# A hybrid trunk on one core: the power of qs, the clearing of Z and the additions on G are put in other places of the queues

## The chip, the core and the metric

The kernel runs on one core of a Trainium2 chip. The metric is device time in microseconds for one whole execution: lower is better. A core has TensorE (PE), whose queue also loads weights (PEld), VectorE (DVE), ScalarE (ACT), GpSimd (POOL) and SyncE (SP). Each takes its instructions in the order in which they were queued for it, and waits for other engines and for DMAs through semaphores.

## What is computed

Two layers of a decoder trunk in float32, sequence 512, width 1024. Each layer has a mixer (eight heads of dilated attention beside four heads of a gated delta rule, one input and one output projection) and a gated feed-forward part. The part around the change is the delta rule. Cut from the reference:

```python
qkv = jax.nn.silu(causal_dwconv(dn_qkv, dn_conv_w)).astype(jnp.float32)
...
q = q * lax.rsqrt(jnp.sum(q * q, axis=-1, keepdims=True) + EPS) * (K ** -0.5)
k = k * lax.rsqrt(jnp.sum(k * k, axis=-1, keepdims=True) + EPS)
...
g = jnp.cumsum(g, axis=-1)
decay = jnp.exp(jnp.where(tril, g[..., :, None] - g[..., None, :], -jnp.inf))
A = jnp.where(strict, jnp.einsum('bhnik,bhnjk->bhnij', kb, k) * decay, 0.0)
T = lax.linalg.triangular_solve(A + eye, jnp.broadcast_to(eye, A.shape), left_side=True,
                                lower=True, unit_diagonal=True)
...
def step(state, xs):
    v_new = u_i - jnp.einsum('bhck,bhkv->bhcv', w_i, state)
    o = jnp.einsum('bhck,bhkv->bhcv', q_i, state) + jnp.einsum('bhij,bhjv->bhiv', qk_i, v_new)
    state = state * gl[..., None, None] + jnp.einsum('bhck,bhcv->bhkv', k_i, v_new)
...
dn_out = (rms_norm(o, dn_norm_w) * jax.nn.silu(z)).reshape(B, S, DELTA_V_WIDTH).astype(h.dtype)
```

## The kernel before

Tokens are handled as four tiles of 128 (t = 0 to 3), which are also the chunks of the delta rule. A dense product is made as three products of split operands, a high and a low part (hh and hl of the activations, wh and wl of the weights); wh is a rounded copy by ScalarE, wl the rest by VectorE, from a loaded piece st. Dense products gather in PSUM tiles pm (4 buffers), all small ones in pw (4 buffers).

Every instruction goes through one helper (line 54), so all rows name L54 and are told apart by their tiles. A tile scheduler orders each engine's queue by a priority: `prio` sets the level, `weave` mixes streams of work by their share of progress (dense projections, `prepare`, `attention`, `invert`, `scan`). Dense work has a late level, the delta rule's chain an early one. What the scheduler finds ready first by its own costs stands first, so an edit also moves instructions that it doesn't name.

The delta rule in order, with the names in the rows:

- `key` and `conv_silu` (lines 373 to 387): a short convolution into acc, ScalarE's tanh into kT, and one VectorE instruction kT<-kT,acc that finishes a head's key. TensorE then transposes it (pw<-ident,kT).
- `decay` (to line 453): the running sums of the decay go to DRAM (dG), and one DMA for each chunk spreads them back over partitions into G. SP issues these.
- `prepare` (lines 461 to 524): norms of the keys (ssk, bb, bd, and sk by a power on GpSimd); for each chunk and head VectorE adds ng and a mask to G (G<-G,ng,dmask), ScalarE takes the exponential, and U is made of G and a product of keys. 32 x 32 diagonal blocks of U (Lb) are inverted by a chain on GpSimd (Xt, X), and the result goes to DRAM (dX).
- `invert` (lines 526 to 582): for two chunks at once, GpSimd issues the DMA of zc from dX and clears zt and the two Z; VectorE transposes zc's 32 x 32 blocks into Z; GpSimd copies zc into zt; TensorE builds the larger blocks from Z and UT (pw<-Z,UT, then pw<-PB,zt).
- `query` and `project2` (lines 637 to 677): the sums of squares of the queries, qs (128 x 16), become rsqrt(sum + 4 EPS) / sqrt(128) by an addition on VectorE, a power of -0.5 on GpSimd and a multiplication on VectorE.
- `scan` (lines 769 to 818): chunk by chunk R<-pw,neg,Vt, TensorE's R,Z into y, the new state S<-S,egl,pw, and the output o.
- `normed` (lines 830 to 845): ScalarE's sums of squares of o scaled by qs (junk<-o,qs in the trace; four for each chunk, into os), os scaled by VectorE, the power of on GpSimd, and dno.

Of the kernel before, what the change touches and what calls it, by code (L numbers as in the profile page):

```python
# [12 lines left out]
AF = mybir.ActivationFunctionType  # L13
OP = mybir.AluOpType
# [3 lines left out]
P = 128  # L18
# [7 lines left out]
H = 4  # L26
DK = 128
FF = 2816
NF = 22
EPS = 1e-6  # L30
NB = 32
# [40 lines left out]
class Engine:  # L72
# [3 lines left out]
    def __getattr__(self, name):  # L76
        f = getattr(self._engine, name)
        return lambda *args, **kwargs: self._engines.issue(f, self._pe, args, kwargs)


def run(gen):
# [5 lines left out]
def hybrid_trunk(ctx: ExitStack, tc: tile.TileContext, a, out):  # L87
    nc = Engines(tc)
# [10 lines left out]
    def const(name, shape):  # L99
        t = cp.tile(shape, F32, name=name)  # L100
        nc.sync.dma_start(t, a[name])
        return t
# [12 lines left out]
    with prio(2.5):  # L115
        cw = const("cw", [P, NL, 12, 4])
        dmask = const("dmask", [P, P])
# [14 lines left out]
    def big(name, dtype=F32, shape=(P, T), tag="b2", bufs=None):  # L132
        return bp.tile(list(shape), dtype, name=name, tag=tag, bufs=bufs)

    def ev(name, dtype=F32, shape=(P, T)):
        return big(name, dtype, shape, "ev", 4)

    def am(name, dtype=F32, shape=(P, T)):
        return big(name, dtype, shape, "am", 4)

    def pair(name, shape=(P, 2, T)):
        return big(name, F32, shape, "b4", 2)
# [19 lines left out]
    def ps4(name="pw", shape=(P, 4, P)):  # L162
        return pw.tile(list(shape), F32, name=name, tag="pw")
# [47 lines left out]
    def square_sum(src, acc, scale=1.0, tag="junk"):  # L211
        junk = sp.tile([P, D if tag == "junk" else T], BF, name="junk", tag=tag, bufs=1)
        nc.scalar.activation(junk[:, :src.shape[-1]], src, AF.Square, scale=scale, accum_out=acc)
# [122 lines left out]
    def s16(name):  # L336
        return sp.tile([P, 16], F32, name=name, bufs=1)

    def v3(t_):
        return t_.rearrange("p (t h) -> p t h", h=H)  # L340
# [4 lines left out]
    for l in range(NL):  # L345
# [27 lines left out]
        def conv_silu(cb, ps, dst):  # L373

            acc = ev("acc")
            nc.scalar.activation(acc, ps, AF.Copy, scale=cw[:, l, cb, 3:4])
            for j in range(1, 4):
                nc.vector.scalar_tensor_tensor(acc[:, j:], ps[:, :T - j], cw[:, l, cb, 3 - j:4 - j], acc[:, j:],
                                               op0=OP.mult, op1=OP.add)
            nc.scalar.activation(dst, acc, AF.Tanh, scale=0.5)  # L380
            nc.vector.scalar_tensor_tensor(dst, dst, 1.0, acc, op0=OP.add, op1=OP.mult)

        kT, qT, Kt, Vt = [], [], [], []

        def key(h, ps):
            kT.append(big("kT"))
            conv_silu(4 + h, ps, kT[h])


        bet, bb, bd, ng, eg, neg, egl, ssk, gr = (s16(n) for n in ("bet", "bb", "bd", "ng", "eg", "neg", "egl", "ssk",  # L390
                                                                    "gr"))
        sk, qs = s16("sk"), s16("qs")
        Gs, UT, Z = [], [], []
# [67 lines left out]
        def prepare():  # L461
            for h in range(H):
                pk = ps4()
                for t in range(NT):
                    nc.tensor.transpose(pk[:, t, :], kT[h][:, t * P:(t + 1) * P], ident)
                Kt.append(big("Kt", shape=(P, NT, P)))
                for t in range(NT):
                    square_sum(pk[:, t, :], v3(ssk)[:, t, h:h + 1])
                sk_h, bb_h, bd_h = (v3(v)[:, :, h] for v in (ssk, bb, bd))
                nc.vector.tensor_scalar(sk_h, sk_h, 4 * EPS, None, op0=OP.add)  # L470
                nc.vector.reciprocal(bb_h, sk_h)
                nc.vector.tensor_tensor(bb_h, bb_h, v3(bet)[:, :, h], op=OP.mult)
                nc.vector.tensor_tensor(bd_h, bd_h, bb_h, op=OP.mult)
                for t in range(NT):
                    i = t * H + h
                    nc.scalar.activation(Kt[h][:, t, :], pk[:, t, :], AF.Copy, scale=bd[:, i:i + 1])
                yield
            nc.vector.tensor_scalar(sk, ssk, 0.25, None, op0=OP.mult)
            nc.gpsimd.tensor_tensor(sk, sk, pexp[:, :16], op=OP.pow)
            yield  # L480

            Lb = pair("Lb", (64, NB, NB))
            X = pair("X", (64, NB, NB))
            nc.sync.dma_start(X.rearrange("p a b -> p (a b)"), a["eye32"])
            for t in range(NT):
                G = Gs[t]
                for h in range(H):
                    i = t * H + h
                    nc.vector.scalar_tensor_tensor(G[:, h, :], G[:, h, :], ng[:, i:i + 1], dmask,
                                                   op0=OP.add, op1=OP.add)  # L490
                nc.scalar.activation(G, G, AF.Exp)
                pu = ps4()
                U = am("U", shape=(P, H, P))
                for h in range(H):
                    ks = kT[h][:, t * P:(t + 1) * P]
                    nc.tensor.matmul(pu[:, h, :], ks, ks, start=True, stop=True)
                for h in range(H):
                    i = t * H + h
                    nc.vector.scalar_tensor_tensor(U[:, h, :], pu[:, h, :], bb[:, i:i + 1], G[:, h, :],
                                                   op0=OP.mult, op1=OP.mult)  # L500
                nc.sync.dma_start(dU[t, :P * H * P].rearrange("(p n) -> p n", p=P), U.rearrange("p h i -> p (h i)"))
                pt = ps4()
                for h in range(H):
                    nc.tensor.transpose(pt[:, h, :], U[:, h, :], ident)
                UT.append(big("UT", shape=(P, H, P)))
                nc.scalar.activation(UT[t], pt, AF.Copy)
                yield

            for h in range(H):
                src = bass.AP(tensor=dU.tensor, offset=dU.offset + h * P,  # L510
                              ap=[[NB * H * P + NB, 16], [H * P, NB], [1, NB]])
                nc.sync.dma_start(Lb[h * 16:h * 16 + 16], src)
            for j in range(NB - 1):
                n = NB - 1 - j
                tmp = xp.tile([64, 256], F32, name="Xt", tag="Xt")
                tv = tmp[:, :n * (j + 1)].rearrange("p (n m) -> p n m", n=n)
                nc.gpsimd.tensor_tensor(tv, Lb[:, j, j + 1:].unsqueeze(2).to_broadcast([64, n, j + 1]),
                                        X[:, j, None, :j + 1].to_broadcast([64, n, j + 1]), op=OP.mult)
                nc.gpsimd.tensor_tensor(X[:, j + 1:, :j + 1], X[:, j + 1:, :j + 1], tv, op=OP.subtract)
                if j % 4 == 3:  # L520
                    yield
            for h in range(H):
                dst = bass.AP(tensor=dX.tensor, offset=dX.offset + h * NB, ap=[[NB * P, 16], [P, NB], [1, NB]])
                nc.gpsimd.dma_start(dst, X[h * 16:h * 16 + 16])

        def invert():

            for t0 in range(0, NT, 2):
                ts_ = range(t0, t0 + 2)
                zc = am("zc", shape=(P, 2, H, NB))  # L530
                nc.gpsimd.dma_start(zc.rearrange("p t h i -> p t (h i)"),
                                    dX[t0 * P:(t0 + 2) * P, :].rearrange("(t p) n -> p t n", p=P))
                zt = xp.tile([64, 2, H, 64], F32, name="zt")
                nc.gpsimd.memset(zt, 0.0)
                for t in ts_:
                    Z.append(big("Z", shape=(P, H, P)))
                    nc.gpsimd.memset(Z[t], 0.0)
                for t in ts_:
                    for r in range(0, P, NB):
                        nc.vector.transpose(Z[t][r:r + NB, :, r:r + NB], zc[r:r + NB, t - t0])  # L540
                for r in (0, NB):
                    nc.gpsimd.tensor_copy(zt[r:r + NB, :, :, r:r + NB], zc[r:r + NB])
                pp = ps4(shape=(P, 2, H, NB))
                pb = ev("PB", shape=(P, 2, H, NB))
                for r in (0, 64):
# [16 lines left out]
                for t in ts_:  # L562
                    for r in (0, 64):
                        nc.vector.tensor_scalar(Z[t][r:r + 32, :, r + 32:r + 64], po[r:r + 32, t - t0], -1.0, None,
                                                op0=OP.mult)
# [60 lines left out]
        def at_proj(s, evac):  # L626
            return tok_proj(lambda pc: load_w(a["w_at"][l, s, pc], [2, T]), 4, act_h, 2, evac)
# [42 lines left out]
        def project2():  # L670
            yield from chan_proj(lambda b: a["w_dn"][l, 8 + b], 4, 0, delta_value)
            yield from chan_proj(lambda b: a["w_dn"][l, b], 4, 0, query, (), lambda b: nc.gpsimd if b > 1 else None)
            with prio(*CHAIN):
                nc.vector.tensor_scalar(qs, qs, 4 * EPS, None, op0=OP.add)
                nc.gpsimd.tensor_tensor(qs, qs, pexp[:, 16:], op=OP.pow)
                nc.vector.tensor_scalar(qs, qs, DK ** -0.5, None, op0=OP.mult)
            yield from at_proj(3, gate)

        heads = []
# [425 lines left out]
```

## Time and profile before

| | us |
|---|---|
| median of 3 runs | 1341.43 |
| range of these runs | 1341.21 to 1342.85 |
| profiled execution | 1338.06 |
| its span in the trace | 1336.3 |
| TensorE busy | 1298.1 |
| VectorE busy | 1005.6 |
| ScalarE busy | 724.8 |
| GpSimd busy | 182.5 |

A row of a timeline reads: start, duration (from the first start to the last end, where several instructions are joined), engine, line, operation, output<-inputs, shapes, count, and in brackets the idle time of the engine before it with what ended that. A row of TensorE's waits reads: the waiting work <- what it waited for: us in total, times, longest. Engines start the next instruction a little before the printed end of the one ahead, so the distance of two starts is what an instruction costs its queue.

### The profile page before, as it was taken

How to read it: one execution, taken by the hardware profiler on the slowest of the kernel's cores; microseconds unless marked ns; L12 is line 12 of the kernel's file. 1: busy time of each engine (PE TensorE's matmuls, PEld its weight loads, DVE VectorE, ACT ScalarE, POOL GpSimd, SP SyncE). 2: the span in 40 equal slices, each digit the busy share in tenths (PEclk: the TensorE clock that was granted, in tenths of full speed). 3: DMA queues.
4: the chain of work that ended last, by engine and by line, in shares of the span. 5: the costliest groups of instructions: out<-in, count | busy, mean ns of one | idle time of the engine just before them, and what ended most of it. 6: DMA issues, size and time to landing. Idle time of an engine off the chain costs nothing.

```text
span 1336.3 us, 19288 instructions
## 1 busy us (share of the span) xinstructions
PE 1298.1 (97%) x6892; PEld 1082.3 (81%) x6892; DVE 1005.6 (75%) x1940; ACT 724.8 (54%) x1458; POOL 182.5 (14%) x230
## 2 busy tenths in 40 slices
PE   8999999999999999999999999999999999999997
PEld 7787878888888888888777877888888888888876
DVE  6756878868576778788777668889667667888885
ACT  5635966755333444467546359667553334444673
POOL 0019410101000000030010293002110000001201
PEclk9999999999999999999999999999999999999999
DMA  7233211253366566356652332203435565653664
GB/s 238 85 103 96 71 52 37 67 177 120 139 228 222 183 220 206 116 178 187 212 174 72 110 96 61 66 17 115 138 127 192 195 228 190 222 187 109 199 187 160
DMA packets 75425, 193.14 MB, mean 145 GB/s; under 512 B 13345, under 2 KB 13889, under 8 KB 75330
## 3 DMA queue, kind: packets, MB, share of 16 engines
q1 hardware_dynamic: 74882, 190.87, 44.4%
q0 software_dynamic: 448, 1.05, 0.4%
q8 instruction: 54, 0.88, 0.3%
q14 instruction: 41, 0.34, 0.1%
HBM read 161.99 MB, written 29.90 MB: 144 GB/s over the span
## 4 chain that ended last, share of the span: by engine, by line
PE 79%; DVE 8%; ACT 5%; DMA 3%; POOL 2%; issue 2%; SPq 0%; POOLq 0%; DVEq 0%; ACTq 0%
PE pm L54 66%; PE pw L54 13%; DVE wl L54 2%; DVE xs L54 1%; ACT wh L54 1%; DVE x L54 1%; POOL nr L54 1%; ACT junk L54 1%; ACT sc L54 1%; DVE hl L54 1%; DMA st<-in_w_f 1%; POOL pr L54 1%; DVE xf L54 1%; ACT Vt L54 0%; DVE KL L54 0%
## 5 line engine op out<-in xcount | busy, mean ns | idle before, releaser
L54 DVE TENSOR_TENSOR wl<-st,wh 128x1024 fp32r<-128x1024 f32 (+1 forms) x250 | 282.3, 1135 | 165.6 <-ACT wh L54 164.5
L54 PE MATMUL pm<-hh,wh 128*128 128x512 f32 (+1 forms) x1024 | 372.5, 366 | 4.7 <-ACT hh L54 4.7
L54 ACT ACTIVATE wh<-st 128x1024 fp32r<-128x1024 f32 (+1 forms) x254 | 245.5, 971 | 239.2 <-PE pm L54 217.5
L54 PE MATMUL pm<-hh,wl 128*128 128x512 f32 (+1 forms) x1024 | 373.0, 366 | 1.1 <-DVE wl L54 1.1
L54 PE MATMUL pm<-hl,wh 128*128 128x512 f32 (+1 forms) x1024 | 373.6, 367 | 0.0
L54 PEld LDWEIGHTS pm<-hh,wh 128*128 128x128 f32 x1024 | 193.7, 190 | 35.4 <-ACT hh L54 6.0
L54 PEld LDWEIGHTS pm<-hh,wl 128*128 128x128 f32 x1024 | 194.3, 191 | 30.8 <-DVE wl L54 1.3
L54 PEld LDWEIGHTS pm<-hl,wh 128*128 128x128 f32 x1024 | 194.4, 191 | 29.2
L54 PE MATMUL pm<-wh,xf 128*128 128x512 f32 x528 | 164.4, 390 | 0.0
L54 PE MATMUL pm<-wh,hh 128*128 128x512 f32 x384 | 153.4, 402 | 0.0
L54 PE MATMUL pm<-wl,hh 128*128 128x512 f32 x384 | 152.5, 399 | 0.0
L54 PE MATMUL pm<-wh,hl 128*128 128x512 f32 x384 | 151.3, 396 | 0.0
L54 DVE SCALAR_TENSOR_TENSOR fgu<-pm,fw,fgu 128x511 f32<-128x511 f32 (+1 forms) x176 | 131.2, 746 | 22.0 <-ACT fgu L54 19.9
L54 PEld LDWEIGHTS pm<-wh,xf 128*128 128x128 f32 x528 | 99.1, 188 | 21.2 <-ACT e L54 0.6
L54 PE MATMUL pm<-wl,xf 128*128 128x512 f32 x264 | 103.6, 392 | 0.5 <-DVE wl L54 0.5
L54 POOL TENSOR_TENSOR g<-g 128x256 f32<-128x256 f32 x22 | 25.4, 1173 | 493.1 <-DVE xf L54 493.1
L54 PEld LDWEIGHTS pm<-wh,hl 128*128 128x128 f32 x384 | 72.4, 189 | 14.2
L54 PEld LDWEIGHTS pm<-wh,hh 128*128 128x128 f32 x384 | 72.0, 188 | 14.4 <-DVE zs L54 0.6
L54 PEld LDWEIGHTS pm<-wl,hh 128*128 128x128 f32 x384 | 72.5, 189 | 13.7 <-DVE wl L54 0.8
L54 ACT ACTIVATE xf<-g 128x256 fp32r<-128x256 f32 x154 | 60.4, 411 | 33.9 <-PE pm L54 22.3
L54 ACT ACTIVATE fgu<-fgu 128x512 f32<-128x512 f32 x44 | 27.8, 632 | 91.8 <-DVE fgu L54 89.2
L54 ACT ACTIVATE fgu<-pm,fb,fw 128x512 f32<-128x512 f32 x88 | 66.9, 761 | 18.6 <-PE pm L54 18.6
(228 smaller groups left out, 1798.7 us busy)
## 6 DMA issues: line engine op xcount, KB each, us to landing
st<-in_w_f SPq DMA_DIRECT2D x118, 512.0 KB, 3.7
ws<-in_w_f SPq DMA_DIRECT2D x88, 256.0 KB, 4.6
T<-ws SPq DMA_DIRECT2D x66, 256.0 KB, 2.3
st<-in_w_at SPq DMA_DIRECT2D x32, 512.0 KB, 3.8
st<-T SPq DMA_DIRECT2D x30, 512.0 KB, 4.1
st<-in_w_dn SPq DMA_DIRECT2D x24, 512.0 KB, 3.8
st<-in_w_out SPq DMA_DIRECT2D x16, 512.0 KB, 3.7
U<-ws SPq DMA_DIRECT2D x22, 256.0 KB, 2.3
```

The lines of the kernel that those rows point to most:

```text
L54: r = f(*args, **kwargs)
```

## The change

Three edits in the mixer. In the **power of qs**, VectorE adds 4 EPS and multiplies by 128 in one instruction ahead of GpSimd's power, and the multiplication behind the power is gone. **Z** of the first two chunks is taken and cleared at the end of `prepare`; the other two are cleared in `invert` as before, and the zt copies are done by ScalarE. The **additions on G** carry a rule that they are queued behind the last key's final instruction.

```diff
+@contextmanager
+def behind(tc, ins):
+    if ins is None:
+        yield
+    else:
+        with tc.issue_after(ins.ins):
+            yield
...
             nc.scalar.activation(dst, acc, AF.Tanh, scale=0.5)
-            nc.vector.scalar_tensor_tensor(dst, dst, 1.0, acc, op0=OP.add, op1=OP.mult)
-
-        kT, qT, Kt, Vt = [], [], [], []
+            return nc.vector.scalar_tensor_tensor(dst, dst, 1.0, acc, op0=OP.add, op1=OP.mult)
+
+        kT, qT, Kt, Vt, keyed = [], [], [], [], []
 
         def key(h, ps):
             kT.append(big("kT"))
-            conv_silu(4 + h, ps, kT[h])
+            keyed.append(conv_silu(4 + h, ps, kT[h]))
...
-                for h in range(H):
-                    i = t * H + h
-                    nc.vector.scalar_tensor_tensor(G[:, h, :], G[:, h, :], ng[:, i:i + 1], dmask,
-                                                   op0=OP.add, op1=OP.add)
+                with behind(tc, keyed[-1]):
+                    for h in range(H):
+                        i = t * H + h
+                        nc.vector.scalar_tensor_tensor(G[:, h, :], G[:, h, :], ng[:, i:i + 1], dmask,
+                                                       op0=OP.add, op1=OP.add)
...
                 nc.gpsimd.dma_start(dst, X[h * 16:h * 16 + 16])
+            cleared(range(2))
+
+        def cleared(ts_):
+            for t in ts_:
+                Z.append(big("Z", shape=(P, H, P)))
+                nc.gpsimd.memset(Z[t], 0.0)
...
-                for t in ts_:
-                    Z.append(big("Z", shape=(P, H, P)))
-                    nc.gpsimd.memset(Z[t], 0.0)
+                if t0:
+                    cleared(ts_)
...
                 for r in (0, NB):
-                    nc.gpsimd.tensor_copy(zt[r:r + NB, :, :, r:r + NB], zc[r:r + NB])
+                    nc.scalar.activation(zt[r:r + NB, :, :, r:r + NB], zc[r:r + NB], AF.Copy)
...
-                nc.vector.tensor_scalar(qs, qs, 4 * EPS, None, op0=OP.add)
+                nc.vector.tensor_scalar(qs, qs, 4 * EPS, float(DK), op0=OP.add, op1=OP.mult)
                 nc.gpsimd.tensor_tensor(qs, qs, pexp[:, 16:], op=OP.pow)
-                nc.vector.tensor_scalar(qs, qs, DK ** -0.5, None, op0=OP.mult)
```

What the scheduler makes of it is seen in the queues. VectorE around the last key of layer 1 (r is the rotated key of the attention), before:

```order
L54 TENSOR_TENSOR bd<-bd,bb 128x4
L54 SCALAR_TENSOR_TENSOR G<-G,ng,dmask 128x128 x2
L54 SCALAR_TENSOR_TENSOR kT<-kT,acc 128x512
L54 SCALAR_TENSOR_TENSOR G<-G,ng,dmask 128x128 x4
L54 TENSOR_TENSOR wl<-st,wh 128x1024
L54 SCALAR_TENSOR_TENSOR G<-G,ng,dmask 128x128 x3
```

and after:

```order
L54 TENSOR_TENSOR bd<-bd,bb 128x4
L54 SCALAR_TENSOR_TENSOR kT<-kT,acc 128x512
L54 SCALAR_TENSOR_TENSOR G<-G,ng,dmask 128x128 x4
L54 TENSOR_TENSOR wl<-st,wh 128x1024
L54 SCALAR_TENSOR_TENSOR G<-G,ng,dmask 128x128 x3
```

Two additions that stood ahead of the key now stand further back, behind the next rows (the first of r among them); in layer 0 nine additions stood ahead of the key, some of them between the small instructions on bb and bd, and none does now.

GpSimd around the DMAs of zc, layer 0, the difference of the two queues (- before, + after):

```order
 L54 DMA zc<-dX 128x2x128
 L54 TENSOR_TENSOR wl<-st,wh 128x1024
+L54 DMA zc<-dX 128x2x128
+L54 MEMSET zt 64x512
 L54 MEMSET Z 128x512 x2
-L54 COPY zt<-zc 32x8x32 x2
-L54 DMA zc<-dX 128x2x128
-L54 MEMSET Z 128x512
-L54 MEMSET zt 64x512
-L54 MEMSET Z 128x512
-L54 COPY zt<-zc 32x8x32 x2
```

The two memsets that are left here belong to the second pair of chunks; those of the first pair now stand behind the power of sk, ahead of the chain on Xt and X, and the copies are on ScalarE. On TensorE the products pw<-PB,zt of the first pair move ahead a little, and 13 dense products instead of 8 stand between the small work and the first pw<-Z,UT of the second pair.

ScalarE around the power of qs, layer 0, the difference of the two queues:

```order
 L54 ACTIVATE zs<-pm 128x512
+L54 ACTIVATE junk,os<-o,qs 128x128
 L54 ACTIVATE wh<-st,dnw 128x1024
-L54 ACTIVATE junk,os<-o,qs 128x128 x6
+L54 ACTIVATE junk,os<-o,qs 128x128 x5
 L54 ACTIVATE at<-pw 64x256
 L54 ACTIVATE junk,os<-o,qs 128x128 x2
```

One of the sums of squares, which read the finished qs, has moved ahead of wh. On VectorE the row qs<-qs between zs and R is gone, and the rows around it keep their order.

## The prediction

> **What bounds the kernel now.** I read the page first (busy shares and the chain that ended last), then TensorE's list of waits, then the timelines around the places that the change touches.
>
> ```profile
> PE 1298.1 (97%) x6892; PEld 1082.3 (81%) x6892; DVE 1005.6 (75%) x1940; ACT 724.8 (54%) x1458; POOL 182.5 (14%) x230
> PE 79%; DVE 8%; ACT 5%; DMA 3%; POOL 2%; issue 2%; SPq 0%; POOLq 0%; DVEq 0%; ACTq 0%
> ...
> PE pw L54 <- POOL zt L54: 3.6, 2, 1.8
> PE pw L54 <- DVE R L54: 2.9, 2, 1.5
> PE pw L54 <- DVE kT L54: 2.8, 2, 2.5
> PE pw L54 <- DVE Z L54: 0.8, 2, 0.4
> ```
>
> TensorE (PE) is busy for 97% of the span, so the change can win only where TensorE stands still. The last four lines are its stalls at the places that the change touches (total, count, longest): 3.6 + 2.9 + 2.8 + 0.8 = 10.1 us in both layers together. Had every one of them gone, the gain would be 10.1 us, 0.75% of the run. No engine's work shrinks by more than a few tenths of a us, so what matters is which wait comes next at each place.
>
> **The last key (G's additions moved behind it).**
>
> ```profile
> 61.52 0.65 PE L54 MATMUL pw<-ident,kT 128*128 128x128 f32 x4 [0.35 <-DVE kT L54]
> ...
> 718.38 0.62 ACT L54 ACTIVATE kT<-acc 128x512 f32<-128x512 f32 x1
> ...
> 721.69 0.61 DVE L54 SCALAR_TENSOR_TENSOR G<-G,ng,dmask 128x128 f32<-128x128 f32 x2 [2.39 <-DMA G<-dG]
> 722.23 0.68 DVE L54 SCALAR_TENSOR_TENSOR kT<-kT,acc 128x512 f32<-128x512 f32 x1
> ...
> 727.32 0.68 DVE L54 TENSOR_TENSOR r<-r,r 128x512 f32<-128x512 f32 x1
> ...
> 722.97 0.65 PE L54 MATMUL pw<-ident,kT 128*128 128x128 f32 x4 [2.49 <-DVE kT L54]
> ...
> 728.25 0.27 PE L54 MATMUL pw<-ident,r 128*128 128x128 f32 x1
> ```
>
> In layer 1 VectorE (DVE) stood idle for 2.39 us, waiting for the DMA of G, with the key's last instruction queued behind the two additions that needed it. That instruction's other input, ScalarE's tanh, was done at 718.38 + 0.62 = 719.00, when VectorE was just free (721.69 - 2.39 = 719.30). In its new place kT starts at about 719.3 and is done near 720.0. TensorE had arrived at 722.97 - 2.49 = 720.48, so the stall of 2.49 goes whole. What is late next is TensorE's transpose of r at 728.25, which would come at 725.76. VectorE's r ended at 727.32 + 0.68 = 728.00. It still waits for G's DMA until 721.69, but between then and r it has less to do: kT (722.83 - 722.23 = 0.60, with the next instruction's start) and two additions that now stand behind r (0.54). So r is ready at 728.00 - 1.14 = 726.86 and TensorE waits 1.1 there. Net **-1.4**, with ends at -2.5 (r not waited for) and 0 (all passed on). In layer 0 nine additions leave the way of kT, and the stall there is 0.35: **-0.35**. G's exponentials on ScalarE come later by these additions; their reader U stands further back, and TensorE's wait for it is in the lower end above.
>
> **The inverse (Z cleared early, zt copied on ScalarE).**
>
> ```profile
> 168.72 0.75 POOL L54 DMA_DIRECT2D zc<-dX  x1 [5.22 <-PE pw L54]
> 169.49 2.40 POOL L54 TENSOR_TENSOR wl<-st,wh 128x1024 fp32r<-128x1024 f32 x1
> 171.81 1.01 POOL L54 MEMSET Z<- 128x512 f32 x2
> 172.75 0.86 POOL L54 COPY zt<-zc 32x256 f32<-32x256 f32 x2
> ...
> DMA to landing us min/median/max: 2.5/2.5/2.6
> ...
> 172.39 2.55 DVE L54 STREAM_TRANSPOSE Z<-zc 32x128 f32<-32x128 f32 x8 [2.08 <-POOL Z L54]
> ...
> 173.15 0.22 PE L54 MATMUL pw<-Z,UT 32*32 32x32 f32 x2 [1.80 <-POOL zt L54]
> ...
> 208.53 0.39 PE L54 MATMUL pm<-wh,hl 128*128 128x512 f32 x1
> 208.75 0.39 PE L54 MATMUL pm<-wh,hh 128*128 128x512 f32 x1
> ```
>
> zc lands at 168.72 + 2.5 = 171.22, but VectorE's transposes into Z begin at 172.39, after the first memset on GpSimd (POOL), which stood behind 2.40 us of wl. TensorE follows the second transpose (2.55 / 8 = 0.32 each, so two end near 173.0, and TensorE starts at 173.15); the page names zt, which merely ended last. With Z cleared long before, the transposes start at the landing: 172.39 - 171.22 = 1.17 earlier, and the stall of 1.80 shrinks to 0.63. The same stands in layer 1 (3.6 in two waits). **-1.17 x 2 = -2.3.** It can be no more than 1.8 x 2, and nothing if the landing is later than its 2.5.
>
> The two zt copies cost ScalarE about 0.4 each (0.86 for two on POOL, the nearest row), ahead of a pTh and a Q that nobody reads before Z's block is done. The pTh product also needs pTl, which stands behind the transposes on VectorE and comes earlier by as much as they do. Between 0 and 0.8 per layer; I take 0. The early memsets (1.01 for two) lie on a POOL that waits there for the DMA of Lb. For the second pair of chunks the stalls are 0.8 together, and TensorE now has five more dense products ahead of the wait (13 instead of 8); at 208.75 - 208.53 = 0.22 each they cover the 0.4 of each stall. **-0.8.** This part: -3.1.
>
> **The slow clock behind that stall.** A table by stretches: start and end, length, busy time of PE, PEld, DVE, ACT and POOL with counts, then the granted clock of TensorE (third from the end).
>
> ```profile
> 173.15:181.65 8.50, 8.49 (x60) 7.02 (x61) 7.02 (x18) 4.43 (x9) 0.40 (x2) 0.80 0.14 58
> 834.85:843.35 8.50, 8.49 (x104) 7.06 (x105) 8.09 (x20) 5.94 (x12) 0.39 (x1) 1.00 0.17 64
> 175.79:179.20 3.41, 3.41 (x14) 3.02 (x13) 2.90 (x7) 1.48 (x4) 0.00 (x0) 0.50 0.00 0
> ```
>
> After the same stall, 8.5 us ran at a granted clock of 0.80 in layer 0 and at 1.00 in layer 1; the slow piece is 3.41 us at 0.50, that is 1.7 us of work lost. A stall of 0.63 is less likely to bring it on, but what decided between two equal stalls the profile does not show. Between 0 and -1.7; I take the middle, **-0.8**. [...]
>
> **The power of qs (no VectorE work behind it).**
>
> ```profile
> 256.47 2.93 POOL L54 TENSOR_TENSOR qs<-qs,pexp 128x16 f32<-128x16 f32 x1 [18.81 <-DVE qs L54]
> 262.61 1.92 POOL L54 TENSOR_TENSOR of<-os,pexp 128x4 f32<-128x4 f32 x1 [3.20 <-DVE os L54]
> 265.06 1.01 POOL L54 TENSOR_TENSOR of<-os,pexp 128x4 f32<-128x4 f32 x1 [0.53 <-DVE os L54]
> ...
> 257.26 0.69 DVE L54 SCALAR_TENSOR_TENSOR zs<-zs,pm 128x512 f32<-128x512 f32 x1 [0.24 <-ACT zs L54]
> 259.44 0.17 DVE L54 TENSOR_SCALAR qs<-qs 128x16 f32<-128x16 f32 x1 [1.50 <-POOL qs L54]
> 262.37 0.16 DVE L54 TENSOR_SCALAR os<-os 128x4 f32<-128x4 f32 x1
> 262.44 1.22 DVE L54 TENSOR_TENSOR wl<-st,wh 128x1024 fp32r<-128x1024 f32 x1
> 263.70 1.12 DVE L54 SCALAR_TENSOR_TENSOR S<-S,egl,pw 128x128 f32<-128x128 f32 x4
> 266.45 1.12 DVE L54 SCALAR_TENSOR_TENSOR R<-pw,neg,Vt 128x128 f32<-128x128 f32 x4
> ...
> 257.11 1.15 ACT L54 ACTIVATE wh<-st,dnw 128x1024 fp32r<-128x1024 f32 x1
> 259.65 0.40 ACT L54 ACTIVATE junk<-o,qs 128x128 bf16<-128x128 f32 x1 [1.39 <-DVE qs L54]
> 262.80 0.38 ACT L54 ACTIVATE at<-pw 64x256 f32<-64x256 f32 x1
> ...
> 259.92 1.01 PE L54 MATMUL pw<-R,Z 128*128 128x128 f32 x6 [1.42 <-DVE R L54]
> 265.29 1.06 PE L54 MATMUL pw<-S,kT 128*128 128x128 f32 x8
> 266.94 0.46 PE L54 MATMUL pw<-R,Z 128*128 128x128 f32 x2
> ```
>
> Without the multiplication, R follows zs at about 257.9 instead of 259.5, and TensorE's stall of 1.42 goes (1.50 in layer 1). But ScalarE's order changes with it. Before, wh (1.15) stood ahead of the first sum of squares and ran inside the wait for qs. Now that sum stands first and waits for POOL until 256.47 + 2.93 = 259.40, with wh queued behind it. The sums have a pitch of (262.80 - 259.65) / 6 = 0.525; os needs four. Before they were done at 259.65 + 4 x 0.525 = 261.75, and VectorE came to os only at 262.37. Now: 259.40 + 0.05 + 4 x 0.525 + 1.15 = 262.7. VectorE, 1.6 us early, waits there for it, and behind os on its queue stand wl, S and the next R, all **0.33 later** than before. TensorE's gain of 1.42 is lost in two steps: it reaches S,kT at 263.87 and waits for S (263.70 + 0.33, and the first of four), and it reaches the next R,Z with R at 266.45 + 0.33, so at 267.27 instead of 266.94. VectorE's rows show no idle time from 259.44 to 266.45, so nothing there makes the 0.33 good. **+0.33 x 2 = +0.7**, with ends at -1.5 and +1.15 (all of wh) per layer.
>
> **Sum**, against the profiled run of 1338.06 (span 1336.3 and 1.8 around it): -1.75 - 3.1 - 0.8 + 0.7 = -4.95, so 1333.1. The median of the three runs shown, 1341.43, lies 3.4 above that execution; I carry the difference over: **1336.5**.
>
> **Rivals.**
> 1. **The qs part works whole**: os is not late, because VectorE reaches it no earlier than 262.7, held by TensorE's other products. Then both R stalls go, -2.9 instead of +0.7: 1332.9. Against it stands the order of ScalarE and VectorE above.
> 2. **The stalls only move**: layer 1's kT wait comes back whole at r, and half of the Z gain is lost behind zt on ScalarE, the clock staying as it is. Left: -0.35 - 1.15 - 0.8 + 0.7 = -1.6, so 1339.8, no difference to speak of. For it: TensorE's waits on VectorE follow one another closely here.
> 3. **Slower: POOL's power stretches** when VectorE runs R beside it instead of waiting. For it: a power of 128x4 took 1.92 with wl beside it and 1.01 without, a ratio of 1.9; 2.93 would become 5.6, and os, wl and S come 2.6 later still, in both layers: -4.95 + 5.3 = +0.4, or +1.2 if the clock stays too, 1342.6. It decides the sign from a stretch of about 2.5 per layer. Against it: zs and o ran beside the 2.93 already, with one operand in PSUM as R has. [...]
>
> **How the numbers follow.** My forecast 0.55, rival 1 0.15, rival 2 0.22, rival 3 0.08. The likeliest time is 1336.5; its own range, from the unknown ends (clock 1.7, r 1.1, wh 1.6), is 1334 to 1339. To hold 8 in 10 the range must take in rivals 1 and 2: **1332.5 to 1340.5**. About 0.2%, 2.7 us, is what a measurement of this kernel can tell from no change: faster means below 1338.7. The forecast is nearly all there (0.53), rival 1 whole: faster 0.70; same 0.24; slower 0.06.
>
> **What would show it.** In the new profile TensorE's wait for kT should be gone in both layers, with a wait of about 1 us for r in layer 1; the first Z,UT stall should be near 0.6 with transposes starting at the landing; R,Z should have no wait at the second chunk, but os on VectorE a wait of about 1.7 on ScalarE's sums, and S,kT or the third R,Z a new one. A granted clock of 1.00 around 175 us would confirm that term. The prediction is wrong if os is not waited for (then faster), if pow rows are far above 2.9 (slower), or if slow clock pieces appear elsewhere.

## The result, and the profile after

| | before | changed |
|---|---|---|
| median beside each other | 1341.87 (4 runs) | 1331.40 (4 runs) |
| ratio, 95% interval | | 0.9934 (0.9913 to 0.9954) |
| profiled execution | 1338.06 | 1331.07 |
| its span | 1336.3 | 1329.3 |
| mean and count of all later runs (changed: with the four above) | 1340.0, 57 | 1332.6, 14 |

The change makes the kernel faster, by 0.5 to 0.9% in the first comparison and by 7.4 us on the means in the last row. The forecast was 1336.5, 4.9 less than the median shown then. The sign and the places were right, the size was too small: the first median lies below the range's low end of 1332.5, and that of the next ten runs, 1332.3, just below it; as a ratio on the median shown then, 0.9934 x 1341.43 = 1332.6, it lies just inside. One execution of e7 below took 1832.68 at a granted clock of 0.656 and is left out of its ratio and of all means.

TensorE's waits in the profile after, with the columns as before (in total, times, longest):

```profile
PE pw L54 <- DVE S L54: 2.1, 2, 1.0
PE pw L54 <- DVE R L54: 0.8, 2, 0.4
PE pw L54 <- DVE Z L54: 0.7, 1, 0.7
PE pw L54 <- POOL wl L54: 0.7, 1, 0.7
PE pw L54 <- ACT G L54: 0.4, 1, 0.4
```

The 3.6 at zt have become 1.4 (the rows Z and wl are the first pw<-Z,UT of one layer each), the 0.8 of the second pair and the 2.8 at kT are gone, with 0.4 left at r. But of the 2.9 at R, 0.8 stands there still, and 2.1 at S is new: the two make up what was removed. TensorE's busy time is the same within 0.6 us (1297.5 after 1298.1), and its idle time, span less busy time, falls by 6.4 (38.2 to 31.8). The four places make 5.4 of that (10.1 before, 4.7 now). One more wait is gone that the prediction didn't list, on the key product of the queries some 15 us behind the first Z,UT. Its row before:

```profile
PE pw L54 <- DVE qT L54: 0.6, 2, 0.3
```

This row is the same in e1 and e2 below and is in no list of a kernel with the edit of Z. The rest are small waits that differ between executions. Both profiled executions have a granted clock of 0.996, so none of their 7.0 us is the clock.

The places themselves, from the timelines after. The last key of layer 1 (VectorE, ScalarE, TensorE):

```profile
716.75 1.14 DVE L54 SCALAR_TENSOR_TENSOR G<-G,ng,dmask 128x128 f32<-128x128 f32 x4 [0.93 <-DMA G<-dG]
...
721.26 0.68 DVE L54 TENSOR_TENSOR r<-r,r 128x512 f32<-128x512 f32 x1
...
721.38 0.63 ACT L54 ACTIVATE G<-G 128x512 f32<-128x512 f32 x1 [0.54 <-DVE G L54]
...
716.26 0.60 PE L54 MATMUL pw<-ident,kT 128*128 128x128 f32 x4
722.09 0.30 PE L54 MATMUL pw<-ident,r 128*128 128x128 f32 x1 [0.43 <-ACT G L54]
```

TensorE no longer waits for kT. VectorE's wait for G's DMA is still there, now behind the key, and what it delays is r: r ends 721.94 - 716.75 = 5.19 after that wait, where the prediction had 726.86 - 721.69 = 5.17. TensorE's row names ScalarE's exponential of G, which ended at 722.01, 0.07 behind r. Which of the two TensorE waited for can't be told from this; both stand behind the additions on G.

The inverse, layer 0:

```profile
167.60 0.75 POOL L54 DMA_DIRECT2D zc<-dX  x1 [5.24 <-PE pw L54]
...
170.14 2.55 DVE L54 STREAM_TRANSPOSE Z<-zc 32x128 f32<-32x128 f32 x8 [1.58 <-DMA zc<-dX]
...
170.90 0.22 PE L54 MATMUL pw<-Z,UT 32*32 32x32 f32 x2 [0.66 <-POOL wl L54]
```

The transposes follow the landing (170.14 - 167.60 = 2.54) and name the DMA as what they waited for. The stall is 0.66, where the prediction had 0.63. Its row names GpSimd's wl, which ended at 170.77, as the second transpose did (170.14 + 2 x 0.32); in layer 1 the stall of 0.71 names Z.

The power of qs, layer 0 (VectorE, ScalarE, GpSimd, TensorE):

```profile
255.47 0.69 DVE L54 COPY y<-pw 128x512 f32<-128x512 f32 x1
257.82 0.17 DVE L54 TENSOR_SCALAR os<-os 128x4 f32<-128x4 f32 x1 [1.66 <-ACT junk L54]
...
254.81 0.40 ACT L54 ACTIVATE junk<-o,qs 128x128 bf16<-128x128 f32 x1 [2.21 <-POOL qs L54]
255.12 0.19 ACT L54 ACTIVATION_READ_ACCUMULATOR junk<-o,qs 128x1 f32 x1
255.21 1.14 ACT L54 ACTIVATE wh<-st,dnw 128x1024 fp32r<-128x1024 f32 x1
256.25 0.39 ACT L54 ACTIVATE junk<-o,qs 128x128 bf16<-128x128 f32 x1
...
251.85 2.93 POOL L54 TENSOR_TENSOR qs<-qs,pexp 128x16 f32<-128x16 f32 x1 [18.72 <-DVE qs L54]
...
253.71 0.93 PE L54 MATMUL pw<-R,Z 128*128 128x128 f32 x6
260.20 1.16 PE L54 MATMUL pw<-S,kT 128*128 128x128 f32 x8 [1.04 <-DVE S L54]
262.45 0.46 PE L54 MATMUL pw<-R,Z 128*128 128x128 f32 x2 [0.39 <-DVE R L54]
```

This is the chain that the prediction described: the first R,Z has no wait, wh runs behind the first sum, VectorE waits 1.66 for os, and TensorE gives its gain back in 1.04 at S,kT and 0.39 at the next R,Z. The power lasts 2.93 as before, with R (253.24 to 254.36 on VectorE) beside it.

### The profile page after: what moved, and what is told of

Read it like the earlier page. It is cut to its first block, busy times and chain, and to the rows that moved or that the text cites. A ratio compares the mean times of both kernels' runs of the same rounds, so it can differ in the third digit from the quotient of the medians.

```text
span 1329.3 us, 19287 instructions
## 1 busy us (share of the span) xinstructions
PE 1297.5 (98%) x6892; PEld 1082.3 (81%) x6892; DVE 1005.4 (76%) x1938; ACT 728.0 (55%) x1466; POOL 179.4 (13%) x222
## 4 chain that ended last, share of the span: by engine, by line
PE 72%; DVE 6%; ACT 3%; issue 2%; POOL 2%; DMA 1%; POOLq 0%; DVEq 0%; ACTq 0%; SPq 0%
PE pm L54 62%; PE pw L54 10%; DVE wl L54 2%; ACT junk L54 1%; DVE xs L54 1%; DVE x L54 1%; POOL nr L54 1%; DMA st<-in_w_f 1%; ACT wh L54 1%; DVE xf L54 1%; POOL pr L54 1%; DVE hl L54 0%; POOL qs L54 0%; ACT sc L54 0%; DMA G<-dG 0%
```

## The experiments

Two theories had to be told apart for each part: that the three parts are worth what their own stalls show, and that the size came from somewhere else (the clock, or qs working after all). Each of the first four kernels has one part alone, or two without the third.

**One part alone, and the change without qs.** e1 is the kernel before with this edit only:

```diff
-                nc.vector.tensor_scalar(qs, qs, 4 * EPS, None, op0=OP.add)
+                nc.vector.tensor_scalar(qs, qs, 4 * EPS, float(DK), op0=OP.add, op1=OP.mult)
                 nc.gpsimd.tensor_tensor(qs, qs, pexp[:, 16:], op=OP.pow)
-                nc.vector.tensor_scalar(qs, qs, DK ** -0.5, None, op0=OP.mult)
```

e2 has only the lines with `behind`, e3 only those on Z and zt, e4 all but those on qs.

> Before with the edit of qs alone. Theory (the sums of squares on ScalarE now hold wh behind them, so VectorE waits for os and TensorE for S and the next R): TensorE's wait for R at the second chunk (1.42 and 1.50) is gone, VectorE waits about 1.7 us for os, TensorE about 1.0 for S,kT and 0.4 for the next R; net +0.1 to +0.3 us per layer, the time within 1 us of before. Rival (the edit works whole): no wait for os, 2.9 us faster than before.

> Before with the additions on G behind the last key, and nothing else. Theory: both waits of TensorE for kT are gone (0.35 and 2.49), and what is late next in layer 1 is a wait of 0.4 us for r, not the 1.1 of the prediction; about -2.7 us against before in the trace. Rival (the prediction's term): -1.75. Rival (a stall that only moves): under -1.

> Before with Z of the first pair cleared early and zt copied on ScalarE, and nothing else. Theory: the stalls ahead of the first Z,UT shrink from 1.80 to about 0.65 in both layers, those of the second pair go; -2.3 and about -1.1, in sum -3.4 us in the trace, and on top of it 1.7 us for each run of slow clock behind the long stall that no longer occurs (up to two in an execution), so the median 4 to 6 us below before, with granted clocks higher by 0.001 to 0.003. Rival (no link of stall and clock): -3.4 in the median, the same clocks as before.

> The changed kernel without the edit of qs. Theory: the edit of qs brings nothing, so this is as fast as the changed kernel or up to 0.5 us faster: about 0.993 of before. Rival (the edit of qs brought 2.9 us): 0.9955 of before or slower.

| kernel | runs | median | ratio to before, 95% interval |
|---|---|---|---|
| e1, qs alone | 12 | 1340.82 | 1.0006 (0.9994 to 1.0018) |
| e2, G alone | 12 | 1338.48 | 0.9993 (0.9978 to 1.0008) |
| e3, Z and zt alone | 10 | 1334.43 | 0.9958 (0.9943 to 0.9972) |
| e4, all but qs | 6 | 1333.44 | 0.9946 (0.9929 to 0.9963) |

The edit of qs brings nothing that the times show. Its trace shows the same rows as after (TensorE's waits of e1):

```profile
PE pw L54 <- DVE S L54: 2.1, 2, 1.1
PE pw L54 <- DVE R L54: 0.8, 2, 0.4
```

From the start of the power (256.47 before, 251.85 after) to the third chunk's R,Z (266.94 and 262.45) it took 10.47 before and 10.60 in the changed kernel: a loss of 0.13, where the prediction had 0.33. The rival in which qs works whole has fallen, and e4, which lacks the edit, is not slower than the whole change.

G alone can't be told from no change in the times, but its trace is clear: no wait for kT in either layer, and these two rows in layer 1:

```profile
725.50 1.14 DVE L54 SCALAR_TENSOR_TENSOR G<-G,ng,dmask 128x128 f32<-128x128 f32 x4 [1.48 <-DMA G<-dG]
...
PE pw L54 <- ACT G L54: 1.0, 1, 1.0
```

With G's DMA 1.48 late the wait at r is 1.0, as the prediction had it (1.1); with 0.93 in the first profile after it was 0.43. My expectation of 0.4 for e2 was taken from that one trace and was wrong. The traces with this edit have waits of 0.3 to 0.6 where G's DMAs landed in 4.1 to 4.6 (after, e4, e6, e8, e10) and of 1.0 at 5.0 and 5.2 (e2, e5); out of line is 0.9 at 4.6 (e7). What differs is the DMA itself, here by the median from issue to landing of G's four DMAs, in the profile after and in e2:

```profile
DMA to landing us min/median/max: 3.8/4.2/4.4
...
DMA to landing us min/median/max: 4.5/5.0/5.1
```

Z and zt carry most of the gain. The stalls ahead of e3's first Z,UT are 0.81 and 0.76, where about 0.65 was expected. In its list of waits the 4.4 of zt and Z have become 1.6 and the 0.6 of qT is gone, 3.4 in sum, but its time falls by 5.7 in the medians, within the 4 to 6 that were expected with the clock; its mean clock is 0.0017 higher. So the rest leads to the clock.

**The changed kernel again, and the clock.** Three kernels with other edits ran beside this one.

> The changed kernel once more, beside the two that follow. Theory (mean over many runs): 0.9945 to 0.995 of before, about 1333.5, since before's own median over 27 runs is 1340.1; no run of slow clock behind the first Z,UT in either layer. Rival (the clock falls at any place): slow clock at 170 to 182 or 830 to 842 us here too.

e5: 1332.32 median of 10 runs, ratio 0.9948 (0.9930 to 0.9965). But a slow piece stands behind the first Z,UT of layer 1 in its trace, after a stall of only 0.74 (stretches of 8.5 us from that product on, e5's from 0.13 ahead of it; the columns as in the prediction, the granted clock third from the end). First the profile after, layer 0 and 1, then e5, layer 1:

```profile
170.90:179.40 8.50, 8.49 (x89) 6.96 (x90) 8.01 (x20) 7.17 (x15) 0.00 (x0) 1.00 0.22 64
827.28:835.78 8.50, 8.50 (x88) 6.96 (x89) 8.00 (x20) 7.16 (x15) 0.00 (x0) 1.00 0.22 65
...
829.85:838.35 8.50, 8.37 (x59) 7.03 (x60) 7.03 (x18) 5.58 (x12) 0.00 (x0) 0.80 0.22 63
```

So a short stall doesn't rule the slow clock out; the theory as I had put it for e5 is refuted. What is left is a matter of frequency. Behind the first Z,UT, the profiles of the three kernels with the stall of 1.80 (before, e1, e2) have a slow piece in 4 of 6 layers; those with a stall of 0.66 to 0.84 (after, e3 to e8 and e10) in 3 of 16. If the stall made no difference, a split at least this uneven would come about once in 19. The times agree: within a kernel, each 0.001 of mean granted clock goes with 1.03 us (least squares over the 133 runs of eight kernels, each about its own mean), and the kernels' mean clocks differ.

| kernel | runs | mean us | mean clock | mean put to a clock of 0.995 |
|---|---|---|---|---|
| before | 57 | 1340.0 | 0.9940 | 1339.0 |
| e1, qs alone | 12 | 1341.3 | 0.9933 | 1339.6 |
| e2, G alone | 12 | 1338.9 | 0.9932 | 1337.1 |
| e3, Z and zt alone | 10 | 1334.1 | 0.9957 | 1334.8 |
| e4, all but qs | 6 | 1332.6 | 0.9953 | 1332.9 |
| changed | 14 | 1332.6 | 0.9961 | 1333.7 |

At one clock the parts are +0.6, -1.9 and -4.2, in sum -5.5, and the whole change -5.3; the clock adds -2.1 to it. The standard errors of the means are 0.3 for before and 0.5 to 0.7 for the others (0.2 and 0.3 to 0.5 by the scatter about the fit), so the sum holds, while the +0.6 of qs can't be told from the 0.1 per layer of the trace.

The traces give about as much for the clock: behind the first Z,UT the clock is at half for 5.7 us per execution in the mean of before, e1 and e2 and for 1.3 in that of the eight with the edit of Z, and 4.4 us less at half the clock are 2.2 us of work. In the rest of the span, but for its last 6 us, it is 8.0 and 6.8, mostly near TensorE's waits for hh and xs at about 315 and 970 us. The pair of profiles above is an exception: the slow piece at 175.79 is gone, but one stands at 970.78 that before doesn't have. That the edit of Z goes with a higher clock is shown (0.9958 in the mean of the 52 runs of the changed kernel, e3, e4, e6, e7 and e10, 0.9938 in the 81 of before, e1 and e2); that it does so by the shorter stall rests on the few pieces counted above and is not shown as a mechanism, and what decides in a single case stays open.

**wh ahead of the sums again.** If os is what holds S and the next R, ScalarE's order alone should bring R's gain back.

```diff
             for h in range(H):
-                square_sum(o[:, h, :], os_[:, h:h + 1], qst[:, h:h + 1])
+                with prio(*(URGENT if t else (L + 1, L + 4.3))):
+                    square_sum(o[:, h, :], os_[:, h:h + 1], qst[:, h:h + 1])
```

> The changed kernel with the first chunk's sums of squares at a lower priority, so that wh stands ahead of them on ScalarE again. Theory: os is ready 1.1 us earlier, VectorE's wait for it falls from 1.66 to about 0.6, TensorE's waits for S,kT (1.04) and the next R (0.39) go or fall below 0.4; 0.9 us per layer, about 1.9 us faster than the changed kernel. Rival (os is not what holds S and R): the waits for S and R stay and the time is the same within 0.5.

e6: 1331.04 median of 6 runs, 0.9929 (0.9900 to 0.9957). Its rows on VectorE and TensorE, layer 0:

```profile
257.88 0.17 DVE L54 TENSOR_SCALAR os<-os 128x4 f32<-128x4 f32 x1 [0.75 <-ACT junk L54]
...
260.26 1.16 PE L54 MATMUL pw<-S,kT 128*128 128x128 f32 x8
262.51 0.46 PE L54 MATMUL pw<-R,Z 128*128 128x128 f32 x2 [0.40 <-DVE R L54]
```

The wait for os falls from 1.66 to 0.75, and that for S goes. The wait for R stays at 0.40. So the order of ScalarE is what took most of the gain: from the start of the power (252.81) to the third chunk's R,Z it takes 9.70 now, 0.9 less than in the changed kernel. Run a second time, beside e9, it came out the same.

> The kernel of e6 once more, beside e9. Theory: 1.9 us below the changed kernel's 1332.5 on the mean, so 1330.6, 0.993 of before.

e10: 1330.96 median of 5 runs, 0.9927 (0.9914 to 0.9940). Over its 11 runs the mean is 1330.6, 2.0 below the changed kernel's 1332.6 with a standard error of 0.8: this version is the fastest one measured, though the intervals of the two against before still overlap.

**No wait for the power at all.**

```diff
-        sk, qs = s16("sk"), s16("qs")
+        sk, qs, q2 = s16("sk"), s16("qs"), s16("q2")
...
+                nc.vector.reciprocal(q2, qs)
                 nc.gpsimd.tensor_tensor(qs, qs, pexp[:, 16:], op=OP.pow)
...
-                square_sum(o[:, h, :], os_[:, h:h + 1], qst[:, h:h + 1])
+                square_sum(o[:, h, :], os_[:, h:h + 1])
...
+            nc.vector.tensor_tensor(os_, os_, q2[:, t * H:(t + 1) * H], op=OP.mult)
             nc.vector.tensor_scalar(os_, os_, 1.0 / DK, EPS, op0=OP.mult, op1=OP.add)
```

> The changed kernel with the sums of squares of o taken without qs, and os multiplied by a reciprocal of qs's argument on VectorE (one more instruction of 0.16 for each chunk and one of 0.2 per layer). ScalarE then has no wait for the power at all. Theory: no wait for os, R's gain of 1.4 stays in both layers, 2.5 to 2.9 us faster than the changed kernel. Rival (the sums, now earlier on ScalarE, hold back pTh and o there): a new wait of TensorE on ScalarE's o or on y, and less than 1 us gained.

e7: 1332.24 median, 0.9945 (0.9928 to 0.9962), the same as the changed kernel. The rival won, though not at the place it named: the wait for R is gone and that for S falls to 0.5 in both layers together, but new ones come, on the product that reads pTl and on the transposes of dno. Its list of TensorE's waits:

```profile
PE pw L54 <- DVE dno L54: 1.8, 2, 0.9
PE pw L54 <- DVE pTl L54: 1.4, 2, 0.7
PE pw L54 <- DVE S L54: 0.5, 2, 0.2
```

**The zt copies.** e8 is the changed kernel with both zt copies on GpSimd as before.

> The changed kernel with the zt copies back on GpSimd; Z is still cleared early. Theory: VectorE's transposes start at the landing of zc all the same, the stall ahead of the first Z,UT is 0.65 in both layers, and the copies, which end some 4 us before their first reader, cost nothing on either engine: the trace within 0.5 us of the changed kernel's. Rival: the copies hold the queue of GpSimd or of ScalarE and the stall differs by over 0.3.

One run, 1332.84. GpSimd's copy starts at 168.96, and TensorE's first Z,UT has about the same wait as with the copies on ScalarE:

```profile
169.26 0.22 PE L54 MATMUL pw<-Z,UT 32*32 32x32 f32 x2 [0.77 <-DVE Z L54]
```

So the shorter stall is owed to the early memsets, and for it it does not matter which engine copies zt.

**zc in a buffer of its own.** What is left ahead of the first Z,UT is zc's landing, and GpSimd issues that DMA only when a buffer of the attention's scores is free (5.24 of idle time ahead of it). e9 is e6 with zc in the buffer of Xt, which is free once the chain on X is done.

```diff
-                tmp = xp.tile([64, 256], F32, name="Xt", tag="Xt")
+                tmp = xp.tile([P, 2, H, NB], F32, name="Xt", tag="Xt").rearrange("p t h i -> p (t h i)")[:64]
...
-                zc = am("zc", shape=(P, 2, H, NB))
+                zc = xp.tile([P, 2, H, NB], F32, name="zc", tag="Xt")
```

> The kernel of e6 with zc in the buffer of Xt instead of one that the attention's scores share, so that its DMA is issued as soon as dX is written. Theory (the 0.66 and 0.75 left ahead of the first Z,UT are zc's landing, 2.5 us behind an issue that waits for a buffer): no wait for zc's landing in either layer, 1.4 us less than e6, and no slow clock at 165 to 182 or 825 to 842 us. Rival (the order moves and VectorE's eight transposes, 0.32 each, hold the next products): a new stall of TensorE on Z or pTl of 0.5 to 1 us in each layer and the same time as e6.

e9: 1369.07, ratio 1.0212 (1.0198 to 1.0226), 29 us slower than before and 38 slower than e6's kernel beside it. TensorE, ScalarE, VectorE and GpSimd in layer 0:

```profile
155.84 0.77 PE L54 MATMUL pw<-pT,va 128*128 128x256 f32 x2 [15.19 <-DVE mx L54]
...
151.71 0.84 ACT L54 ACTIVATE zt<-zc 32x256 f32<-32x256 f32 x2 [15.40 <-DMA zc<-dX]
152.57 0.49 ACT L54 ACTIVATE pTh<-pw 128x384 fp32r<-128x384 f32 x1
...
151.72 1.56 DVE L54 STREAM_TRANSPOSE Z<-zc 32x128 f32<-32x128 f32 x5 [14.40 <-DMA zc<-dX]
...
143.81 2.73 POOL L54 DMA_DIRECT2D dX<-X  x4 [0.31 <-POOL X L54]
149.03 0.74 POOL L54 DMA_DIRECT2D zc<-dX  x1 [2.50 <-DMA dX<-X]
```

Neither theory had this. The zt copies and the transposes now stand ahead of the attention's work in their queues; presumably the scheduler, without the shared buffer, took zc to be ready far earlier than it is. zc is issued at 149.03 and both engines stand for some 15 us at the head of their queues, in each layer. By this the buffer that zc waited for had also held its readers back. An order with zc's own buffer and its readers kept late was not tried.

## Why the prediction was right, and where its sizes were off

- **Last key.** Right: kT's wait went, VectorE's wait for G stayed and passed to r. The -1.4 for layer 1 is what a G landing 5.0 us after its issue gives (a wait of 1.0 at r); in the first profile after it landed in 4.2 and the wait was 0.43. At one clock, G alone is worth -1.9, against -1.75.
- **Inverse.** Right in place and size: 0.66 and 0.71 left of 1.80 (0.63 was predicted), and no wait at the second pair. At one clock -4.2 with a standard error of 0.4 to 0.7, where the term was -3.1; the wait for qT, 0.6 in both layers, went with it, and no term had it.
- **Power of qs.** The mechanism was right step by step, and the rival in which it works whole, at 0.15, fell. The +0.33 per layer was too large, since it took wh at its printed duration of 1.15 and a full pitch for the first sum. In the queue the sum to wh is 255.21 - 254.81 = 0.40 and wh to the next sum 256.25 - 255.21 = 1.04; os came 0.26 earlier than the sum said, and the loss was 0.13.
- **Slow clock.** This is the term that was mis-sized. I took half of one slow piece in one layer, -0.8, from the one profile of before; that a shorter stall makes it less likely was my estimate, and e5 has a slow piece after a stall of 0.74. By the clocks of its other runs (0.9940 in the mean, 0.996 in that profile) and the profiles of e1 and e2, the slow pieces are more frequent without the edit of Z (behind the first Z,UT in 4 of 6 layers, against 3 of 16), and one stands behind the kT stall too (e1, at 726 to 730), so the changed kernel's higher clock is worth -2.1 in the mean. The prediction also named slow pieces elsewhere as a sign of being wrong. One came, at 970.78, and in the profiled pair it cancelled the piece that went. In seven of the eight profiles with the edit of Z one starts between 968 and 976 and before, e1 and e2 have none there; why is not known.
- **Carrying over to the median.** I added 3.4, the distance of the profiled execution from the median of three runs. The mean of 57 runs of before lies 1.9 above that execution, and before's runs spread over 1335 to 1346; three runs were too few for such an offset. This and the clock are most of the difference.
- **The slower rival.** The power stayed at 2.93 with R beside it, so the ratio of 1.9 that this rival took from the two powers on 128 x 4 (1.92 with wl beside, 1.01 without) did not carry over. wl has both inputs in SBUF and R has one in PSUM; that this is what decides was not shown.

## What to carry to other kernels

When a wait is taken away, read what the scheduler now puts at the head of each queue behind it: here one sum of squares moved ahead of a 1.04 us copy and gave back the whole of a 1.4 us stall, and a line of priority brought 0.9 of it back in each layer. Clearing Z far ahead of its use took 1.1 us off a stall each time; its two memsets, 0.99 us in layer 0 of the profile after, ran on a GpSimd that then stood idle for 25.46 us until the DMA of Lb. A buffer that a DMA has to wait for can also be what keeps its readers in a good place in their queues (in e9, without it, engines stood for some 15 us in each layer); before freeing it, look at where the readers go.

## What the runs showed of the hardware

Stalls of TensorE of 0.66 to 1.80 us, with small products of 32 x 32 right behind, were followed by 3.41 us at half the clock (6.83 in one case), not each time: 4 of 6 after 1.80 us, 3 of 16 after 0.66 to 0.84. The same DMA of G took 4.1 to 5.2 us (medians) from issue to landing in different executions. GpSimd's power on 128 x 4 took 1.92 when VectorE's wl, with both inputs in SBUF, had started before it (262.61 in before), 1.38 when the shorter hl (0.69, both inputs in SBUF) had (269.52), and 1.01 when neither had (265.06), though a dno of 0.35 with both inputs in SBUF started inside this last one.
